# A hybrid attention and expert-retrieval layer on one core: sparse tiles normalised where each ends, the last four expert groups taken tile by tile

## The chip, the cores and the metric

The kernel runs on one core of one Trainium2 chip. The metric is the device time of one execution in microseconds (us), as the median of several runs. The engines are called as in the profile: PE is TensorE, whose weight loads stand apart as PEld, DVE is VectorE, ACT is ScalarE, POOL is GpSimd, and SP issues most of the DMAs.

## The reference

One layer over 1024 tokens of width 1024, all in f32. The first part (projection, gated linear attention, windowed attention, output projection and a layer norm) is not touched by the change. The second part is an expert mixer. Each token has 8 heads that each choose 16 of 16384 experts, so 128 chosen experts in all, and then a residual and a last layer norm follow:

```python
u = peer_u[eidx]
v = peer_v[eidx]
act = jax.nn.gelu(jnp.einsum('pd,phkd->phk', xt, u))
peer = jnp.einsum('phk,phkd->pd', gate * act, v)
x = _layernorm(alpha * x + g2 * peer, ln2_g[i], ln2_b[i])
```

## The kernel before, in words

The 1024 tokens are 8 tiles of 128. The kernel does the expert mixer in two ways at once.

**Dense tiles.** Tiles 0 to 4 (640 tokens) multiply with all 16384 experts, in 128 groups of 128. For each group `jj`, `products` loads the group's u-vectors, splits them into a high and a low part (ACT copy L901, DVE subtraction L902) and makes 2 x 24 matmuls of 320 columns (L115 to L117). `gated` applies Gelu (L1075), multiplies with the gates (L1077) and splits the result into the weights `W`. Every JG = 2 groups `outputs` loads the v-vectors through `values` (split by ACT L110 and DVE L111) and makes, for each of 5 tiles and 2 halves of the width, 6 matmuls of 512 columns into the PSUM tile `pyd`, which DVE adds to `yacc` in SBUF (L1105). The weights of two such pairs fit in SBUF at a time. The dense tokens themselves, `hhD`, stay in SBUF until the last product.

**Sparse tiles.** Tiles 5 to 7 take the 128 chosen experts of each token one by one, 128 steps a tile and 384 in all. A step gathers one row of 8 KB for each token (POOL's indirect DMA, L978, 1 MB), DVE multiplies and sums with the token (L995), ACT takes Gelu (L999) and scales the value half (L1011), and POOL adds it to `ys` (L1012). The gathers land in two rings of UB = 3 slots, six in all. A slot is allocated by `slot`, and `room` says whether one is free in program order. At step 96 of a tile `token` takes two slots to prepare the next tile.

**The order of work.** The program is written as one loop over `jj` (L1126 to L1138). After each half of `products` and each tile of `outputs`, `advance` takes as many sparse steps as are due: the 364 steps left are spread over SHARE = 0.98 of the dense work, measured in units in which a product half counts 0.25 and a pair of output groups counts 1. Each engine runs its own queue in order. A scheduler in the framework orders the instructions of the queues by its own simulation, so program order is not always queue order.

**The ends.** A finished sparse tile is stored to DRAM (`y_d`, L1020). After the products of the last group, `prepare` (L929) loads the three rows g2, l2g and l2b into the place of `hhD[0]`, the five residuals into the place of `hhD[1]`, and loads the stored sparse tiles again. `finish` (L948) then does an end: a product with g2 (L949), the residual and its sum (L951), the norm in `normalise` (L1168 to L1181) and the store (L953). In `normalise`, ACT squares and sums (L1171), POOL takes the power (L1173), and then either two DVE operations follow (L1175 and L1176, where FAST is 1) or one ACT operation, a POOL row (L1180) and another row by DVE or POOL (L1179 to L1181). Before the change FAST is 1 for tiles 3, 4 and 7, and SPLIT puts the g2 product and the last row of tiles 5 and 6 on POOL. The last pair of output groups, 126 and 127, runs tile by tile, each tile's end being written behind its second half.

Of the kernel before, what the change touches and what calls it, by code (L numbers as in the profile page):

```python
# [37 lines left out]
def kernel(ctx: ExitStack, tc: tile.TileContext, A, out):  # L38
# [888 lines left out]
    last, waiting = {}, []  # L927

    def prepare():  # L929

        rows = hd.tile([128, 3, D], F32, name="rows", tag="hhD0")
        base = hd.tile([128, 5, D], F32, name="base", tag="hhD1")
        for j in range(ND):
            if j < 3:
                name, src = (("g2", mod_d[3:4]), ("l2g", A["ln2_g"]), ("l2b", A["ln2_b"]))[j]
                last[name] = rows[:, j]
                spread(rows[:, j], src)
            last[j] = base[:, j]
            nc.sync.dma_start(base[:, j], xh_d[j])
        while waiting:  # L940
            j = waiting.pop(0)
            t, r = slot("late")
            r[0] = False
            nc.sync.dma_start(t[:, 0], y_d[j])
            nc.sync.dma_start(t[:, 1], xh_d[j])
            finish(j, t[:, 0], t[:, 1])

    def finish(j, y, x1):  # L948
        (V, G)[SPLIT[j]].tensor_tensor(y, y, last["g2"], OP.mult)  # L949
        mv = sx.tile([128, 2], F32, name="endmv", bufs=4)  # L950
        V.scalar_tensor_tensor(y, x1, ALPHA, y, OP.mult, OP.add, accum_out=mv[:, 0:1])  # L951
        normalise(nc, mhalf, y, x1, mv, last["l2g"], last["l2b"], FAST[j], (V, G)[SPLIT[j]])
        nc.sync.dma_start(out[128 * j:128 * j + 128, :], y)  # L953

    def sparse_steps():
# [25 lines left out]
        for n, (j, k) in enumerate(seq):  # L981
# [4 lines left out]
            while ahead[0] < len(seq) and ahead[0] - n + len(batch) < UB * len(rings) - (size - 1) and room():  # L986
                fetch()
# [9 lines left out]
            if len(batch) >= size or k == 127:  # L997
# [15 lines left out]
                batch.clear()  # L1013
            if k == 127:
                if last:
                    t, _ = slot("late")
                    nc.sync.dma_start(t[:, 0], xh_d[j])
                    finish(j, ys[j], t[:, 0])
                else:
                    nc.sync.dma_start(y_d[j], ys[j])  # L1020
                    waiting.append(j)
# [61 lines left out]
    def values(jj, n):  # L1083
        raw = ep.tile([128, 512], F32, tag="raw", name="vraw", bufs=7)
        nc.sync.dma_start(raw, A["uv"][128 * jj:128 * jj + 128, D + 512 * n:D + 512 * n + 512])
        hi = ep.tile([128, 512], F32R, name="vhi", bufs=4)
        lo = ep.tile([128, 512], F32R, name="vlo", bufs=4)
# [3 lines left out]
    def outputs(jjs, between):  # L1091
        final = jjs[-1] == NJ - 1
        todo = [(t, n) for t in range(ND) for n in range(2)] if final else [(t, n) for n in range(2) for t in range(ND)]
        for t, n in todo:
# [11 lines left out]
                if final and n:  # L1106
                    finish(t, yacc[:, t], last[t])
# [174 lines left out]
```

## Time and profile before

| what | us |
|---|---|
| median of 3 runs | 3180.56 |
| the three runs | 3179.79 to 3192.82 |
| the profiled execution's own time | 3178.78 |
| its span | 3177.0 |
| last matmul of `products` starts | 3108.87 |
| last matmul of all starts | 3130.82 |

The profiled execution is one run of the program. Its span is measured from its first to its last instruction, and 1.8 us of its time lie around it. Timelines and windows give times from the start of the span. A matmul's duration in the timeline overlaps with that of the next one, so the distance between two starts is what a matmul takes from the PE. "Idle before" names what the engine had waited for.

### The profile page before, as it was taken

The page shows a single profiled execution, that of the slowest core. Times are in us where ns is not written, and L with a number is a line of the kernel's source. Part 1 is how long each engine was busy: PE and PEld are TensorE (multiplying, and loading weights), DVE is VectorE, ACT ScalarE, POOL GpSimd, SP SyncE. Part 2 cuts the span into 40 slices and gives each one's busy share as a digit, 9 for nine tenths or more (in the row PEclk, how much of TensorE's full clock was granted, in tenths as well). Part 3 has the DMA queues.
Part 4 walks back from the last instruction along what each step waited for, and adds up shares of the span by engine and source line. Part 5 has one row for each costly group of instructions (what it writes and reads, how often), then busy time and mean ns, then how long its engine had stood idle before and what let it go on. Part 6 is the DMA issues. An engine that isn't in the chain of part 4 may idle for free. (4 is left out here: it accounts for less than half of the span.)

```text
span 3177.0 us, 48921 instructions
## 1 busy us (share of the span) xinstructions
PE 2829.0 (89%) x16604; PEld 2452.3 (77%) x16604; DVE 2594.7 (82%) x5684; ACT 1574.4 (50%) x3437; POOL 1679.8 (53%) x1111
## 2 busy tenths in 40 slices
PE   6998878879778887788999999999999999999893
PEld 3687756757578886677989888888888888888782
DVE  4318844578799999489988998999988999999898
ACT  3324545342547877734545554454544554445452
POOL 0012301052543543137776766778767777778676
PEclk8999879889889998999999999999999999999996
DMA  9653565646466566668898988989888998988884
GB/s 329 222 186 117 208 223 199 216 168 219 149 217 210 224 257 260 246 201 306 323 328 321 319 308 298 341 315 341 315 314 313 337 337 300 321 306 331 304 290 169
DMA packets 352679, 848.82 MB, mean 267 GB/s; under 512 B 27627, under 2 KB 165611, under 8 KB 299692
## 3 DMA queue, kind: packets, MB, share of 16 engines
q1 hardware_dynamic: 285520, 384.20, 36.9%
q0 software_dynamic: 55296, 402.68, 33.3%
q10 hardware_dynamic: 11612, 58.81, 4.8%
q8 instruction: 131, 2.15, 0.3%
q14 instruction: 120, 0.98, 0.1%
HBM read 745.43 MB, written 100.16 MB: 266 GB/s over the span
## 5 line engine op out<-in xcount | busy, mean ns | idle before, releaser
L1012 POOL TENSOR_TENSOR ys<-ys,uv 128x1024 f32<-128x1024 f32 x362 | 900.9, 2489 | 414.5 <-ACT uv L1011 386.9
L117 PE MATMUL pact<-hhD,ulo 128*128 128x320 f32 x2048 | 633.4, 316 | 48.7 <-DVE ulo L902 31.9
L115 PE MATMUL pact<-hhD,uhi 128*128 128x320 f32 x2048 | 641.5, 314 | 9.6 <-DVE W L111 7.4
L116 PE MATMUL pact<-hhD,uhi 128*128 128x320 f32 x2048 | 638.5, 313 | 0.0
L115 PE MATMUL pyd<-vhi,W 128*128 128x512 f32 x1280 | 515.2, 402 | 46.0 <-DVE yacc L1105 38.8
L978 POOL DMA_INDIRECT uv<-in_uv_dram,ex x384 | 415.5, 1082 | 223.0 <-issue 57.1
L116 PE MATMUL pyd<-vlo,W 128*128 128x512 f32 x1280 | 504.1, 394 | 0.2 <-DVE vlo L111 0.2
L117 PE MATMUL pyd<-vhi,W 128*128 128x512 f32 x1280 | 503.6, 397 | 0.0
L1011 ACT ACTIVATE uv<-uv,w 128x1024 f32<-128x1024 f32 x362 | 396.7, 1144 | 185.8 <-DVE w L1000 131.6
L995 DVE SCALAR_TENSOR_TENSOR uv<-uv,h2p 128x1024 f32<-128x1024 f32 x384 | 463.1, 1209 | 15.7 <-DMA uv<-in_uv_dram,ex 14.2
L1105 DVE TENSOR_TENSOR yacc<-yacc,pyd 128x512 f32<-128x512 f32 x630 | 417.3, 676 | 35.6 <-PE pyd L117 34.8
L117 PEld LDWEIGHTS pact<-hhD,ulo 128*128 128x128 f32 x2048 | 389.8, 192 | 68.8 <-DVE ulo L902 41.4
L115 PEld LDWEIGHTS pact<-hhD,uhi 128*128 128x128 f32 x2048 | 392.9, 192 | 24.4 <-DVE W L111 7.8
L116 PEld LDWEIGHTS pact<-hhD,uhi 128*128 128x128 f32 x2048 | 392.0, 191 | 10.7
L115 PEld LDWEIGHTS pyd<-vhi,W 128*128 128x128 f32 x1280 | 242.3, 189 | 94.5 <-DVE yacc L1105 47.4
L111 DVE TENSOR_TENSOR vlo<-vraw,vhi 128x512 fp32r<-128x512 f32 x256 | 284.0, 1131 | 12.2 <-ACT vhi L110 11.9
L902 DVE TENSOR_TENSOR ulo<-uraw,uhi 128x512 fp32r<-128x512 f32 x228 | 266.5, 1174 | 31.8 <-ACT uhi L901 30.4
L117 PEld LDWEIGHTS pyd<-vhi,W 128*128 128x128 f32 x1280 | 242.4, 190 | 58.4
L116 PEld LDWEIGHTS pyd<-vlo,W 128*128 128x128 f32 x1280 | 243.0, 190 | 39.6 <-DVE vlo L111 0.5
L832 PE MATMUL pgb<-ob,oa 128*128 128x128 f32 x1280 | 196.5, 299 | 51.5 <-ACT ob L828 33.8
L832 PEld LDWEIGHTS pgb<-ob,oa 128*128 128x128 f32 x1280 | 179.0, 202 | 65.7 <-ACT ob L828 50.9
L828 ACT ACTIVATE ob<-wb,gj 128x128 f32<-128x128 bf16 x640 | 210.5, 415 | 11.2 <-DVE wb L810 8.2
(357 smaller groups left out, 5099.9 us busy)
## 6 DMA issues: line engine op xcount, KB each, us to landing
uraw<-in_ut_dram SPq DMA_DIRECT2D x256, 256.0 KB, 5.3
vraw<-in_uv_dram SPq DMA_DIRECT2D x256, 256.0 KB, 8.4
g_d<-gstage ACTq DMA_DIRECT2D x20, 2048.0 KB, 6.4
gload<-g_d SPq DMA_DIRECT2D x32, 1280.0 KB, 13.7
wo<-wo_d SPq DMA_DIRECT2D x64, 512.0 KB, 6.1
wq<-wq_d SPq DMA_DIRECT2D x64, 512.0 KB, 6.6
wt<-in_w_ada_dram SPq DMA_DIRECT2D x48, 512.0 KB, 5.9
wq_d<-wqs SPq DMA_DIRECT2D x16, 512.0 KB, 6.0
```

The costliest lines, as they stand in the source:

```text
L111: eng.tensor_tensor(lo, src, hi.bitcast(F32), OP.subtract)
L115: PE.matmul(out_, l[0], r[0], start=(k == 0), stop=False)
L116: PE.matmul(out_, l[0], r[1], start=False, stop=False)
L117: PE.matmul(out_, l[1], r[0], start=False, stop=(k == n - 1))
L828: S.activation(o[1][:, c], w[:, :, c], AF.Copy, scale=gj[:, q + c:q + c + 1])
L832: PE.matmul(p[:, c::4], o[0][:, h + c], o[1][:, h + c], start=True, stop=True)
L902: lower.tensor_tensor(lo, raw, hi.bitcast(F32), OP.subtract)
L978: G.indirect_dma_start(out=uv[n][0].rearrange("p a d -> p (a d)"), out_offset=None, in_=A["uv"], in_offset=bass.IndirectOffsetOnAxis(ap=ch ...
L995: pin(V.scalar_tensor_tensor(t[:, 0], t[:, 0], 1.0, h2[j], OP.mult, OP.mult, accum_out=w[:, i:i + 1]))
L1011: S.activation(v, v, AF.Copy, scale=wb)
L1012: G.tensor_tensor(ys[j], ys[j], v, OP.add)
L1105: V.tensor_tensor(ya, ya, p, OP.add)
```

## The change

Three things are changed. A sparse tile no longer goes to DRAM. At its step 126 two slots of the rings are taken for the residual and the three rows of the norm, which are loaded then, and at step 127 its end runs at once, with the rows on POOL; the slots of tiles 5 and 6 are given back afterwards, those of tile 7 keep the rows for the dense ends. From step 120 of each sparse tile on, two gathers fewer are fetched ahead. The last four groups of outputs (124 to 127) are no longer two pairs but one pass, tile by tile, after all products and all sparse steps; the split values of groups 126 and 127 lie where `hhD[0]` was and the residuals where `hhD[1]` was. All five dense ends take the form with two DVE operations. SHARE goes from 0.98 to 0.96.

```diff
--- before.py
+++ after.py
@@ -924,33 +924,26 @@
     def spread(row, src):
         nc.scalar.dma_start(row, src.to_broadcast([128, D]))
 
-    last, waiting = {}, []
-
-    def prepare():
-
-        rows = hd.tile([128, 3, D], F32, name="rows", tag="hhD0")
-        base = hd.tile([128, 5, D], F32, name="base", tag="hhD1")
+    last, base, late = {}, {}, {}
+
+    def residuals():
+
+        rows = hd.tile([128, ND, D], F32, name="base", tag="hhD1")
         for j in range(ND):
-            if j < 3:
-                name, src = (("g2", mod_d[3:4]), ("l2g", A["ln2_g"]), ("l2b", A["ln2_b"]))[j]
-                last[name] = rows[:, j]
-                spread(rows[:, j], src)
-            last[j] = base[:, j]
-            nc.sync.dma_start(base[:, j], xh_d[j])
-        while waiting:
-            j = waiting.pop(0)
-            t, r = slot("late")
-            r[0] = False
-            nc.sync.dma_start(t[:, 0], y_d[j])
-            nc.sync.dma_start(t[:, 1], xh_d[j])
-            finish(j, t[:, 0], t[:, 1])
-
-    def finish(j, y, x1):
-        (V, G)[SPLIT[j]].tensor_tensor(y, y, last["g2"], OP.mult)
+            base[j] = rows[:, j]
+            nc.sync.dma_start(base[j], xh_d[j])
+        parts = hd.tile([128, 2 * JG, 2, 512], F32R, name="late", tag="hhD0")
+        for i in range(JG):
+            for n in range(2):
+                late[NJ - JG + i, n] = (parts[:, JG * n + i, 0], parts[:, JG * n + i, 1])
+
+    def finish(j, y, x1, fast, rows):
+        o = x1 if j >= ND else y
+        V.tensor_tensor(y, y, rows["g2"], OP.mult)
         mv = sx.tile([128, 2], F32, name="endmv", bufs=4)
-        V.scalar_tensor_tensor(y, x1, ALPHA, y, OP.mult, OP.add, accum_out=mv[:, 0:1])
-        normalise(nc, mhalf, y, x1, mv, last["l2g"], last["l2b"], FAST[j], (V, G)[SPLIT[j]])
-        nc.sync.dma_start(out[128 * j:128 * j + 128, :], y)
+        V.scalar_tensor_tensor(o, x1, ALPHA, y, OP.mult, OP.add, accum_out=mv[:, 0:1])
+        normalise(nc, mhalf, o, y if j >= ND else x1, mv, rows["l2g"], rows["l2b"], fast, G)
+        nc.sync.dma_start(out[128 * j:128 * j + 128, :], o)
 
     def sparse_steps():
 
@@ -983,7 +976,7 @@
             size = 1 if early else BATCH
             if n == 0 or k == 96 and j < NT - 1:
                 token(j + (k > 0))
-            while ahead[0] < len(seq) and ahead[0] - n + len(batch) < UB * len(rings) - (size - 1) and room():
+            while ahead[0] < len(seq) and ahead[0] - n + len(batch) < UB * len(rings) - (size - 1) - 2 * (k >= 120) and room():
                 fetch()
             if k == 0:
                 row, h2[j] = h2[j], ph.tile([128, D], F32, name="h2p", bufs=1)
@@ -1011,14 +1004,18 @@
                         S.activation(v, v, AF.Copy, scale=wb)
                         G.tensor_tensor(ys[j], ys[j], v, OP.add)
                 batch.clear()
+            if k == 126:
+                ends = [slot("late") for _ in range(2)]
+                (a, _), (b, _) = ends
+                x1 = a[:, 0]
+                last.update(g2=a[:, 1], l2g=b[:, 0], l2b=b[:, 1])
+                nc.sync.dma_start(x1, xh_d[j])
+                for name, src in (("g2", mod_d[3:4]), ("l2g", A["ln2_g"]), ("l2b", A["ln2_b"])):
+                    spread(last[name], src)
             if k == 127:
-                if last:
-                    t, _ = slot("late")
-                    nc.sync.dma_start(t[:, 0], xh_d[j])
-                    finish(j, ys[j], t[:, 0])
-                else:
-                    nc.sync.dma_start(y_d[j], ys[j])
-                    waiting.append(j)
+                finish(j, ys[j], x1, False, last)
+                for _, r in ends:
+                    r[0] = j == NT - 1
             yield
 
     with ExitStack() as gx:
@@ -1083,8 +1080,11 @@
     def values(jj, n):
         raw = ep.tile([128, 512], F32, tag="raw", name="vraw", bufs=7)
         nc.sync.dma_start(raw, A["uv"][128 * jj:128 * jj + 128, D + 512 * n:D + 512 * n + 512])
-        hi = ep.tile([128, 512], F32R, name="vhi", bufs=4)
-        lo = ep.tile([128, 512], F32R, name="vlo", bufs=4)
+        if (jj, n) in late:
+            hi, lo = late[jj, n]
+        else:
+            hi = ep.tile([128, 512], F32R, name="vhi", bufs=4)
+            lo = ep.tile([128, 512], F32R, name="vlo", bufs=4)
         split(hi, lo, raw)
         vals[jj, n] = hi, lo
 
@@ -1104,7 +1104,7 @@
                 else:
                     V.tensor_tensor(ya, ya, p, OP.add)
                 if final and n:
-                    finish(t, yacc[:, t], last[t])
+                    finish(t, yacc[:, t], base[t], True, last)
                 between()
 
     yacc = ep.tile([128, ND, D], F32, name="yacc")
@@ -1132,12 +1132,12 @@
                 acts[jj, h] = p
                 gated(jj, h)
                 advance(0.25)
-        if jj == NJ - 1:
-            prepare()
-        if jj % JG == 0 and jj:
+        if jj % JG == 0 and 0 < jj < NJ - JG:
             outputs(list(range(jj - JG, jj)), lambda: advance(JG / (4 * ND)))
     for _ in steps:
         pass
+    residuals()
+    outputs(list(range(NJ - 2 * JG, NJ)), lambda: None)
 
 
 PIECES = ((0, 1, 0, 8), (1, 1, 0, 4), (2, 2, 0, 2), (4, 4, 0, 1),
@@ -1155,14 +1155,12 @@
 UB = 3
 BATCH = 2
 FIRST = 20
-FAST = (0, 0, 0, 1, 1, 0, 0, 1)
-SPLIT = (0, 0, 0, 0, 0, 1, 1, 0)
 FILL = 3
 JG = 2
 GT = 32
 GG = 4
 GJ = 4
-SHARE = 0.98
+SHARE = 0.96
 
 
 def normalise(nc, mhalf, x, spare, mv, g, b, fast, end):
```

## Rows read from the trace of the kernel before

**Rows 1.** The page: the span, and busy time, share and instructions of each engine.

```profile
span 3177.0 us, 48921 instructions
...
PE 2829.0 (89%) x16604; PEld 2452.3 (77%) x16604; DVE 2594.7 (82%) x5684; ACT 1574.4 (50%) x3437; POOL 1679.8 (53%) x1111
```

**Rows 2.** Windows: width, busy PE PEld DVE ACT POOL (count), PEclk, DMA share, GB/s.

```profile
1900.00:3000.00 1100.00, 1059.46 (x5760) 944.25 (x5759) 1006.03 (x1575) 546.22 (x944) 818.65 (x461) 0.99 0.89 318
...
3109.00:3131.30 22.30, 17.22 (x62) 12.49 (x60) 17.04 (x24) 4.48 (x7) 13.06 (x5) 0.85 0.81 307
3131.30:3177.00 45.70, 0.00 (x0) 0.00 (x0) 38.95 (x47) 14.25 (x19) 28.51 (x15) 0.53 0.23 92
```

**Rows 3.** Waits, 1900 to 3000 us: total, times, longest.

```profile
PE pyd L115 <- DVE yacc L1105: 20.9, 13, 5.5
PE pact L117 <- DVE ulo L902: 19.3, 19, 2.0
```

**Rows 4.** Timeline of PE, 3108 to 3131 us: start, duration, instruction, idle before.

```profile
3108.72 0.31 PE L116 MATMUL pact<-hhD,uhi 128*128 128x320 f32 x1
3108.87 0.31 PE L117 MATMUL pact<-hhD,ulo 128*128 128x320 f32 x1
...
3109.26 0.40 PE L116 MATMUL pyd<-vlo,W 128*128 128x512 f32 x1
3109.49 0.40 PE L117 MATMUL pyd<-vhi,W 128*128 128x512 f32 x1
...
3121.57 0.79 PE L115 MATMUL pyd<-vhi,W 128*128 128x512 f32 x1 [3.60 <-DVE yacc L1105]
...
3130.82 0.39 PE L117 MATMUL pyd<-vhi,W 128*128 128x512 f32 x1
```

**Rows 5.** Timeline of DVE, 3134 to 3177 us.

```profile
3134.07 0.14 DVE L1178 TENSOR_TENSOR endmv<-endmv 128x1 f32<-128x1 f32 x1
3134.14 1.21 DVE L949 TENSOR_TENSOR yacc<-yacc,rows 128x1024 f32<-128x1024 f32 x1
...
3140.69 3.35 DVE L951 SCALAR_TENSOR_TENSOR yacc<-base,yacc 128x1024 f32<-128x1024 f32 x1
...
3156.93 1.22 DVE L951 SCALAR_TENSOR_TENSOR yacc<-base,yacc 128x1024 f32<-128x1024 f32 x1
...
3171.55 1.27 DVE L1176 SCALAR_TENSOR_TENSOR yacc<-yacc,endmv,rows 128x1024 f32<-128x1024 f32 x1
```

**Rows 6.** Timeline of POOL, 3112 to 3150 us.

```profile
3112.51 4.88 POOL L1012 TENSOR_TENSOR ys<-ys,uv 128x1024 f32<-128x1024 f32 x2 [1.99 <-ACT uv L1011]
...
3132.49 0.57 POOL L1173 TENSOR_TENSOR endmv<-endmv,mhalf 128x1 f32<-128x1 f32 x1 [6.03 <-DVE endmv L1172]
...
3142.92 6.59 POOL L1181 TENSOR_TENSOR late<-late,rows 128x1024 f32<-128x1024 f32 x2
```

**Rows 7.** Timeline of ACT in the last end.

```profile
3161.61 1.13 ACT L1171 ACTIVATE base<-yacc,endmv 128x1024 f32<-128x1024 f32 x1
```

**Rows 8.** Groups by line, 1900 to 3000 us: busy us, mean ns, idle before.

```profile
L1012 POOL TENSOR_TENSOR ys<-ys,uv 128x1024 f32<-128x1024 f32 x229 | 571.5, 2496 | 218.6 <-ACT uv L1011 197.1 <-ACT ys L1007 10.9 <-issue 1.1
...
L111 DVE TENSOR_TENSOR vlo<-vraw,vhi 128x512 fp32r<-128x512 f32 x156 | 176.8, 1154 | 8.6 <-ACT vhi L110 8.5
L902 DVE TENSOR_TENSOR ulo<-uraw,uhi 128x512 fp32r<-128x512 f32 x143 | 170.1, 1195 | 7.8 <-ACT uhi L901 6.8
```

**Rows 9.** The tile vraw over the run: duration ns min/median/max, first and last start.

```profile
L111 DVE TENSOR_TENSOR vlo<-vraw,vhi x256: 672/684/3234, 1338.2 to 3111.1; 128x512 fp32r<-128x512 f32 x128
```

**Rows 10.** The store of a finished sparse tile: duration, first and last start.

```profile
L1020 SPq DMA_DIRECT2D y_d<-ys x3: 319/326/327, 1901.6 to 3119.7; - x3
```

**Rows 11.** Timeline of POOL around the preparation of the last sparse tile.

```profile
2363.05 0.94 POOL L978 DMA_INDIRECT uv<-in_uv_dram,ex  x1 [10.72 <-DVE h2s L970]
```

**Rows 12.** Windows of the same stretch, columns as in rows 2.

```profile
2340.00:2362.00 22.00, 22.00 (x118) 19.42 (x117) 16.62 (x29) 8.74 (x16) 6.35 (x4) 1.00 0.74 290
```

**Rows 13.** The tile uv: its gathers from issue to landing, us.

```profile
DMA to landing us min/median/max: 5.3/8.2/12.5
```

## The prediction

> **What bounds the kernel now.** I read the page first, then windows by stage, then the waits of PE in the long stage, then the last 70 us engine by engine. The page shows PE busy for 89% of 3177.0 us and DVE for 82% [rows 1]. That is an average over two situations. In the long dense stage PE is busy for 1059 of 1100 us and DVE for 1006 [rows 2]: PE sets the pace, and the 40.5 us in which it is idle are almost all waits for DVE (20.9 and 19.3 us, [rows 3]). In the last 45.7 us PE has nothing left to do and DVE and POOL do eight norms [rows 2]. So two things count: the stretch from the last product's matmul to the end, 3109.0 to 3177.0, that is 68.0 us, and what the change adds to DVE in the long stage.
>
> In those 68.0 us the reader is to see three things. The last pair of outputs needs 60 matmuls; two starts lie 0.23 us apart [rows 4], so that is 13.8 us of PE, but it took 22.3 us at a granted clock of 0.85 [rows 2], among others because PE sat 3.60 us behind an add of DVE [rows 4]. DVE's residual step took 3.35 us while POOL worked on rows, and 1.22 us without them [rows 5, 6]. And no end was completed in the order of the tiles: DVE still did residual sums at 3140.69 and 3156.93, long after the last matmul at 3130.82 [rows 4, 5].
>
> **The change part by part.** I sum against the profiled span, with T = 3109.0 as the end of the last product.
>
> 1. *Four groups in one pass.* The 60 matmuls of groups 124 and 125, 13.8 us, move behind the last product: it ends 13.8 us earlier, and 120 x 0.23 = 27.6 us follow it instead of 13.8. PE's sum doesn't change. The adds of these groups are 10 instead of 20.
>
> 2. *Start of the pass.* Groups 124 and 125 cover 6 x 0.23 = 1.4 us. The values of 126 and 127 can be split only when `hhD[0]` is free, so ACT's copies and two DVE subtractions of 0.68 us [rows 9] start after the last product. I take a gap of 1.5 us. Below it is 0 (the first values in time); above it 8.5 us, what the last pair lost before (22.3 - 13.8 = 8.5, [rows 2]), which covers a value load or a residual load standing wrongly in SP's queue: the five residual loads wait there for `hhD[1]`, and whatever SP issues behind them waits too.
>
> 3. *Dense ends.* For one tile DVE now does two adds (0.68 each, as the same shape of [rows 9]), the g2 product 1.21, the residual 1.22, two small steps of 0.14, and two operations of 1.27 [rows 5]. That is 6.61 us; starts lie 0.07 us closer than durations say (3134.07 and 3134.14, [rows 5]), which takes off 8 x 0.07, and 6.05 us are left. PE needs 24 x 0.23 = 5.52 us a tile. So each end but the last hides behind the next tile's matmuls, and DVE is 4 x 0.53 = 2.1 us behind at the last one. The chain after the last matmul: 0.68 + 1.21 + 1.22 + 0.14, ACT's square 1.13 [rows 7], 0.14 + 1.27 + 1.27, less five overlaps of 0.07, is 6.7 us, and 0.5 us for handing over to ACT and back, an estimate. POOL's power, 0.57 us [rows 6], lies beside the first of the two last operations. The store came 4.2 us after DVE's last operation (3172.82 to 3177.0, [rows 1, 5]). Together 7.2 + 4.2 = 11.4 us.
>
> 4. *Sparse ends in the long stage.* Each adds to DVE 1.21 + 1.22 + 3 x 0.14 = 2.85 us, in all 8.6 us. Each adds two POOL rows like L1181's (3.3 us with DVE working, [rows 6]). What a POOL row costs DVE is seen in the long stage: subtractions take 1154 and 1195 ns instead of 684 [rows 8, 9], so 156 x 0.470 + 143 x 0.511 = 146 us over 229 POOL adds, 0.64 us each; six rows make 3.8 us. [...] Of 8.6 + 3.8 = 12.4 us I let half reach PE, 6.2, because neither engine is the bound alone (DVE idle 94 of 1100 us, PE 40, [rows 2]); the ends are 0 and 12.4. DMA's bytes stay the same (three stores and three reloads of sparse tiles go, six more row loads come). ACT's extra squares and issues lie in its idle half [rows 2].
>
> 5. *Two slots held.* The trace shows two slots taken once, when a tile is prepared: POOL stood 10.72 us [rows 11], PE stayed busy for all 22 us, and DVE for 16.6 of 22 [rows 12], 3.5 us less than its share in the long stage. Half of that, three times, is 5.2 us; the ends are 0 (PE lost nothing then) and 10.5. With two gathers fewer ahead, three steps of 4.76 us (1901.6 to 3119.7 over 256 steps, [rows 10]) stand against landings of 8.2, at most 12.5 us [rows 13], which still fits.
>
> 6. *SHARE 0.96.* Some seven steps leave the last stretch of the loop and are spread ahead of it. DVE's load rises there and falls behind by the same, each step about 2 us with its POOL add: net 0, ends 0 and +15 if what falls late is not regained.
>
> 7. *Tile 7's end.* Before, step 384 is due 8 pieces of output and one product before T (8 x 1.38 + 48 x 0.15 = 18 us), yet its POOL add ended at 3117.4 [rows 6], 26 us late. Now half a product, ten pieces and three products follow it, 38.4 us, so its add ends some 12 us before the last product, and its end may reach into the pass: 2 us, ends 0 and 7.
>
> Sum: 3109.0 - 13.8 + 6.2 + 5.2 = 3106.6 for the last product, + 1.5 + 27.6 + 2.1 + 11.4 + 2 = **3151.2** against 3177.0, so 25.8 us less. The median of the runs shown is 1.8 us above the profiled execution's own time (3180.56 against 3178.78); I take 25.8 us from the median: **3155 us**.
>
> **The rivals.**
>
> *A. DVE is the pace of the long stage.* For it: every wait of PE there is for DVE. Then the whole 12.4 + 10.5 + 15 = 37.9 us arrive instead of 11.4, and the time is 3181: no change. Against it: PE is busier than DVE. [...] Chance 0.17.
>
> *B. The ends still don't follow the tiles.* The last pair was tile by tile in the program before, too, and DVE's queue was ordered otherwise. If DVE does the finishing of five tiles after the last add, it needs 5 x 4.75 + 6 = 30 us behind PE in place of 13.5, and the time is 3171. Against it: what disordered it, late rows and reloads and POOL rows, is gone. Chance 0.14.
>
> *C. The sparse stream sets the pace.* If steps follow each other as fast as the ring allows, the stream's end stays at 3117.4 plus a pause p for each of tiles 5 and 6; the last product ends 12.4 us later and the span 44.6 us after that, at 3174.4 + 2p. With the 10.7 us of the pause that was seen [rows 11] this is 3195.8, a time of 3199: slower. It decides from p = 9.3 us on. For it: the end holds two slots longer than the preparation does, and DVE works in order, so a late gather stops the adds. Against it: PE ran through that pause. Chance 0.10.
>
> **How the numbers follow.** About 0.5% (16 us) is what a measurement of this kernel can tell from no change, so faster means under 3164.7 and slower over 3196.5. The forecast has 0.52, better than all its upper ends 0.07 (with steps 2, 4, 5 and 7 at their lower ends, 14.9 us less, 3140). Faster: 0.59 and 0.08 from the better parts of A and B, 0.67. Slower: C and a tail of A, 0.11. The rest, 0.22, is the same. The range is 3140 to 3190: its low end is the sum with the lower bounds, its high end takes in A, B and the milder half of C.
>
> **What would show it.** Right: the last product near 3107, matmuls at 0.23 us without a gap to about 3136, DVE's residual steps at 1.2 us in the order of the tiles, and 11 to 14 us between the last matmul and the end. Step 4 or 5 is wrong if PE's waits for DVE grow by more than 20 us, or PE stands still around the ends of tiles 5 and 6. Step 2 is wrong if PE's first wait in the pass is over 4 us or its clock falls. The forecast as a whole fails if the last product ends after 3120 or more than 25 us lie behind the last matmul.

## The result and the profile after

The changed kernel takes 3215.64 us (median of 6 runs, 3202.17 to 3223.82) against 3180.23 us for the kernel before (6 runs): a ratio of 1.0111, 95% interval 1.0086 to 1.0136. It is slower by 35 us where 25.8 us less were forecast, and it lies above the range. The profiled execution's own time is 3219.36 us, its span 3217.6.

The page of the changed kernel, against [rows 1]:

```profile
span 3217.6 us, 48884 instructions
...
PE 2849.5 (89%) x16604; PEld 2460.6 (76%) x16604; DVE 2637.9 (82%) x5675; ACT 1567.8 (49%) x3435; POOL 1673.7 (52%) x1108
```

The windows, with the columns of [rows 2]. The second is the time from the last product to the last matmul, the third what lies behind it:

```profile
1900.00:3000.00 1100.00, 1033.00 (x5538) 916.69 (x5537) 1006.49 (x1515) 523.32 (x908) 779.19 (x440) 0.98 0.85 304
3143.00:3176.20 33.20, 27.27 (x106) 20.51 (x104) 23.20 (x37) 12.98 (x20) 20.09 (x11) 0.90 0.68 269
3176.20:3217.60 41.40, 0.00 (x0) 0.00 (x0) 33.85 (x41) 8.14 (x13) 17.70 (x10) 0.54 0.19 76
```

The first row holds most of the answer. In the same 1100 us PE did 5538 matmuls instead of 5760 and was busy for 1033.0 us instead of 1059.5, while DVE was busy for exactly as long as before (1006.5 against 1006.0), with 60 instructions fewer. So a DVE instruction took longer on average. The waits of PE in that stretch, against [rows 3], and the groups, against [rows 8], say which:

```profile
PE pyd L115 <- DVE yacc L1105: 34.4, 26, 5.0
PE pact L117 <- DVE ulo L902: 30.4, 25, 2.7
```

```profile
L1005 POOL TENSOR_TENSOR ys<-ys,uv 128x1024 f32<-128x1024 f32 x216 | 538.9, 2495 | 251.1 <-ACT uv L1004 241.2 <-issue 1.2
...
L111 DVE TENSOR_TENSOR vlo<-vraw,vhi 128x512 fp32r<-128x512 f32 x150 | 189.9, 1289 | 12.2 <-ACT vhi L110 12.0
L902 DVE TENSOR_TENSOR ulo<-uraw,uhi 128x512 fp32r<-128x512 f32 x138 | 176.4, 1285 | 11.5 <-ACT uhi L901 8.5 <-PE pact L117 2.3
```

The same two waits grew by 24.6 us, and the subtractions from 1154 and 1195 to 1289 and 1285 ns. Above the 684 ns of an undisturbed one that is 150 x 0.605 + 138 x 0.601 = 174 us in the 1100, against 146 before, although POOL did 216 adds there instead of 229: 0.80 us for each add instead of 0.64. I call this sum the **excess** below; it is the number by which the experiments are compared.

By place: the last product began at 3142.7 instead of 3108.9 (forecast 3106.6), and 74.9 us lay behind it instead of 68.1 (forecast 44.6). What happened behind it shows in DVE's timeline, against [rows 5]:

```profile
3171.28 1.21 DVE L988 SCALAR_TENSOR_TENSOR uv<-uv,h2p 128x1024 f32<-128x1024 f32 x1
...
3174.06 8.94 DVE L942 TENSOR_TENSOR yacc<-yacc,late 128x1024 f32<-128x1024 f32 x4
...
3185.79 1.21 DVE L944 SCALAR_TENSOR_TENSOR late<-late,ys 128x1024 f32<-128x1024 f32 x1
...
3186.93 1.22 DVE L944 SCALAR_TENSOR_TENSOR yacc<-base,yacc 128x1024 f32<-128x1024 f32 x1
...
3204.46 1.22 DVE L944 SCALAR_TENSOR_TENSOR yacc<-base,yacc 128x1024 f32<-128x1024 f32 x1
```

The last step of the sparse stream (L988) came at 3171.3, 64 us later than before and inside the pass. Tile 7's residual (the row with `late<-late,ys`) followed at 3185.8, and the first dense residual stands directly behind it, though four dense tiles were summed by 3174. POOL's timeline shows the stream's last add and the two pauses of its gathers (L971) at the ends of tiles 5 and 6:

```profile
1904.96 1.82 POOL L971 DMA_INDIRECT uv<-in_uv_dram,ex  x1 [0.30 <-issue]
1911.04 0.57 POOL L1171 TENSOR_TENSOR endmv<-endmv,mhalf 128x1 f32<-128x1 f32 x1 [4.26 <-DVE endmv L1170]
1914.88 1.00 POOL L971 DMA_INDIRECT uv<-in_uv_dram,ex  x1 [3.27 <-ACT ys L1000]
...
2564.35 1.42 POOL L971 DMA_INDIRECT uv<-in_uv_dram,ex  x1 [0.30 <-issue]
...
2582.74 1.01 POOL L971 DMA_INDIRECT uv<-in_uv_dram,ex  x1 [3.34 <-ACT ys L1000]
...
3174.26 6.52 POOL L1005 TENSOR_TENSOR ys<-ys,uv 128x1024 f32<-128x1024 f32 x2 [7.25 <-ACT uv L1004]
```

From gather to gather 9.9 and 18.4 us went by, where the kernel before had 6.2 and 11.8 at the same places. Gaps of such a length stand elsewhere, too: the longest before is 20.1 us, from 1934.6. The last add ended at 3180.8, 38 us after the last product; the forecast had it 12 us before.

### The profile page after: what moved, and what is told of

Read it like the earlier page. It is cut to its first block, busy times and chain, and to the rows that moved or that the text cites. A ratio compares the mean times of both kernels' runs of the same rounds, so it can differ in the third digit from the quotient of the medians.

```text
span 3217.6 us, 48884 instructions
## 1 busy us (share of the span) xinstructions
PE 2849.5 (89%) x16604; PEld 2460.6 (76%) x16604; DVE 2637.9 (82%) x5675; ACT 1567.8 (49%) x3435; POOL 1673.7 (52%) x1108
## 4 chain that ended last, share of the span: by engine, by line
DVE 33%; PE 29%; issue 10%; ACT 8%; DMA 6%; POOL 1%; SPq 1%; DVEq 0%; ACTq 0%; POOLq 0%
DVE uv L988 5%; DVE vlo L111 5%; DVE ulo L902 4%; DVE yacc L1105 4%; PE pyd L115 4%; PE pact L117 3%; PE pact L116 3%; PE pyd L116 3%; PE pyd L117 3%; PE pact L115 3%; ACT uv L1004 2%; DMA gload<-g_d 2%; DVE oa L824 2%; DVE W L111 1%; PE po_att L576 1%
## 5 line engine op out<-in xcount | busy, mean ns | idle before, releaser
L1005 POOL TENSOR_TENSOR ys<-ys,uv 128x1024 f32<-128x1024 f32 x362 | 904.6, 2499 | 438.6 <-ACT uv L1004 421.4
L115 PE MATMUL pyd<-vhi,W 128*128 128x512 f32 x1260 | 510.3, 405 | 54.5 <-DVE yacc L1105 47.5
L971 POOL DMA_INDIRECT uv<-in_uv_dram,ex x384 | 416.5, 1085 | 230.4 <-issue 57.5
L117 PE MATMUL pyd<-vhi,W 128*128 128x512 f32 x1260 | 497.3, 398 | 1.7 <-DVE W L111 1.7
L116 PE MATMUL pyd<-vlo,W 128*128 128x512 f32 x1260 | 497.2, 395 | 0.0
L988 DVE SCALAR_TENSOR_TENSOR uv<-uv,h2p 128x1024 f32<-128x1024 f32 x384 | 462.3, 1208 | 12.2 <-DMA uv<-in_uv_dram,ex 11.3
L1105 DVE TENSOR_TENSOR yacc<-yacc,pyd 128x512 f32<-128x512 f32 x620 | 410.5, 676 | 30.4 <-PE pyd L117 29.8
L116 PEld LDWEIGHTS pact<-hhD,uhi 128*128 128x128 f32 x2048 | 394.5, 193 | 10.9
L111 DVE TENSOR_TENSOR vlo<-vraw,vhi 128x512 fp32r<-128x512 f32 x252 | 318.8, 1289 | 22.2 <-ACT vhi L110 22.1
L902 DVE TENSOR_TENSOR ulo<-uraw,uhi 128x512 fp32r<-128x512 f32 x228 | 274.2, 1208 | 38.0 <-ACT uhi L901 34.5
L110 ACT ACTIVATE W<-pact 128x320 fp32r<-128x320 f32 x222 | 95.3, 432 | 327.7 <-DVE pact L1074 324.5
```

What stands on the lines that cost most here:

```text
L110: S.activation(hi, src, AF.Copy)
L111: eng.tensor_tensor(lo, src, hi.bitcast(F32), OP.subtract)
L115: PE.matmul(out_, l[0], r[0], start=(k == 0), stop=False)
L116: PE.matmul(out_, l[0], r[1], start=False, stop=False)
L117: PE.matmul(out_, l[1], r[0], start=False, stop=(k == n - 1))
L902: lower.tensor_tensor(lo, raw, hi.bitcast(F32), OP.subtract)
```

## The experiments

Three theories stood after this reading; the expectations below call them by these numbers. Theory 1: the slots held by a sparse end, and the order of the queues behind it, make DVE's subtractions stand behind POOL's adds. Theory 2: SHARE = 0.96 does it alone, by a stream of steps that is 2% denser. Theory 3: the sparse stream has a pace of its own, whatever SHARE says. Letters stand for narrower questions: A and B ask what holds the dense ends (rows that come late, or their place behind tile 7's in DVE's queue), R whether the ring's slots set the stream's pace, L whether POOL's adds are what is lost, S whether the end of the stream and then DVE's ends set the finish.

For each profiled run I give the ratio to the kernel before on the same chip, the excess and PE's busy time in 1900 to 3000 us (before: 146 us and 1059.5 us), and where it matters the length of the long stage, from add 20 to add 590 into `yacc` (before 1598.4 us, after 1654.0). Adds and steps are counted from 0, and the ten copies that open `yacc` count as adds.

**SHARE alone, each way.** The changed kernel with the old value:

```diff
-SHARE = 0.96
+SHARE = 0.98
```

> The changed kernel with SHARE 0.98 again, nothing else. Theory 1 (the slots held by a sparse end, and the order of the queues behind it, make DVE's subtractions stand behind POOL's adds in tile 6's stretch): the long stage stays some 40 to 50 us late and the time near 3215. Theory 2 (a stream of steps 2% denser overloads DVE): most of the loss goes, 3165 to 3185. Theory 3 (the sparse stream has a pace of its own, about 4.75 us a step, whatever SHARE says): the last step stays within 15 us of 3171 and the time within 10 us of 3215.

And the kernel before with the new one:

```diff
-SHARE = 0.98
+SHARE = 0.96
```

> The kernel before with SHARE 0.96, nothing else. Theory 1: no change, 3175 to 3190. Theory 2: 3200 or more. Theory 3: the last step stays within 10 us of 3107, dense work is merely displaced, and the time is within 10 us of 3180.

The changed kernel with 0.98 took 3188.07 us, ratio 1.0031 (1.0014 to 1.0047): stage 1609.4 us, excess 165, PE 1053.3. The kernel before with 0.96 took 3197.17 us, ratio 1.0060 (1.0038 to 1.0081): stage 1632.6 us, excess 160, PE 1048.8. The windows of the two, 0.98 first:

```profile
1900.00:3000.00 1100.00, 1053.32 (x5714) 940.43 (x5713) 1015.92 (x1566) 543.34 (x940) 806.37 (x452) 0.99 0.88 316
```

```profile
1900.00:3000.00 1100.00, 1048.80 (x5652) 933.54 (x5652) 1006.76 (x1543) 538.53 (x926) 800.18 (x449) 0.99 0.87 311
```

3188 lies just above what Theory 2 expected and far from the 3215 of the others; 3197 lies between what Theories 1 and 2 expected. So none of the three holds as it was put: SHARE costs by itself, and the rest of the change isn't free. The groups and waits of the kernel before with 0.96, in the same stretch:

```profile
L902 DVE TENSOR_TENSOR ulo<-uraw,uhi 128x512 fp32r<-128x512 f32 x139 | 182.3, 1322 | 14.1 <-ACT uhi L901 11.4 <-PE pact L117 2.2
L111 DVE TENSOR_TENSOR vlo<-vraw,vhi 128x512 fp32r<-128x512 f32 x154 | 173.2, 1147 | 10.0 <-ACT vhi L110 9.9
```

```profile
PE pact L117 <- DVE ulo L902: 30.5, 25, 3.5
PE pyd L115 <- DVE yacc L1105: 19.7, 16, 2.5
```

One constant moved `ulo` from 1195 to 1322 ns, and PE's wait for it from 19.3 to 30.5 us, with no instruction more. In the long stage 0.96 costs 34 us alone and 45 us with the sparse ends (1654.0 - 1609.4); the sparse ends cost 11 us at 0.98 and 21 at 0.96. Of this less is left at the end of the kernel: by the ratios 0.96 costs 19 us alone (1.0060) and 25 us with the sparse ends (1.0111 against 1.0031).

**Is it how dense the steps stand, or one unlucky order?** The same constant at the values beside it, in the kernel before:

```diff
-SHARE = 0.98
+SHARE = 0.97
```

(and 0.99, 0.95)

> The kernel before with SHARE 0.97. If the loss at 0.96 (3197) comes from steps packed denser, this lies about halfway, 3186 to 3191. If SHARE only draws another order of the queues and the order decides how often DVE's subtractions stand behind POOL's adds: any value from 3165 to 3200, not on that line, and DVE's lost time per POOL add in the three tiles' stretches goes with the time.

> The kernel before with SHARE 0.99. Density: 3170 to 3178, faster than before. Order alone: any value from 3165 to 3200.

> The kernel before with SHARE 0.95. If a smaller SHARE costs more the smaller it is: 3203 or more, DVE's lost time between add 20 and add 590 above the 314 us of share96. If 0.96 is one unlucky order among several: below 3192, with lost time below 305 us. In both cases the steps stand at the same adds as before (591 to 593 adds before step 360).

0.97 gave 1.0018 (1.0005 to 1.0031), excess 148, PE 1059.4; 0.99 gave 0.9981 (0.9964 to 0.9997), 142, 1061.9; 0.95 gave 1.0005 (0.9990 to 1.0020), 145, 1056.6. So 0.96 is worse than the values on both sides of it. A density would grow from 0.99 to 0.95, and this doesn't; 0.97 and 0.99 alone would not decide it (3175.18 lies in both ranges expected for 0.99), but 0.95 came 24 us below what a density asks. And the steps don't get denser: 592 adds were done before step 360 at 0.95, 0.97, 0.98 and 0.99, and 591 at 0.96.

What a value of SHARE changes is the order in which instructions stand in the queues. The traces show it: DVE's instructions from add 20 to add 590 follow each other in another order at each of the five values. Where two kernels have the same order there, they have nearly the same stage. The order, by tile and operation, is the same in the kernel before and in the two kernels with its long stage below (dense ends alone; pass without held slots): 1598.4, 1592.9 and 1593.8 us. It is the same in the four kernels with all sparse ends and 0.98: 1609.1 to 1611.5 us. And it is the same in the two kernels with 0.96 and no sparse end in the stage: 1632.6 and 1632.0 us. The orders of 0.95, 0.97 and 0.99 took 1608.7, 1614.5 and 1610.8 us, so 0.98 was the best of the five here.

**The ends of tiles 5 and 6 left out**, from the changed kernel at 0.96:

```diff
-            while ahead[0] < len(seq) and ahead[0] - n + len(batch) < UB * len(rings) - (size - 1) - 2 * (k >= 120) and room():
+            while ahead[0] < len(seq) and ahead[0] - n + len(batch) < UB * len(rings) - (size - 1) - 2 * (k >= 120 and j == NT - 1) and room():
...
-            if k == 126:
+            if k == 126 and j == NT - 1:
...
-            if k == 127:
+            if k == 127 and j == NT - 1:
```

> The changed kernel without the ends of tiles 5 and 6, which are left out together with their slots and with the shorter fetching ahead; tile 7 and the dense tiles keep theirs. Tiles 5 and 6 are not written. Theory 1: the slow stretch of tile 6 goes, the last product comes near 3095 to 3105 instead of 3142.7, and the time is 3160 to 3175. Theories 2 and 3: the last product stays later than 3125 and the time above 3195.

3172.26 us, ratio 0.9981 (0.9961 to 1.0000). The stage was 1627.3 us, 26.7 less than in the changed kernel, but still 29 above the kernel before: excess 164, PE 1050.0. The last step came at 3118.6 instead of 3171.3, tile 7's residual at 3132.6, the first dense one at 3133.8. The time lies in the range of Theory 1, the last product, at 3117.1, doesn't: it was expected at 3095 to 3105. Without the two ends, 589 adds were done before step 360, with them 599: the two ends, with the slots that they hold, push the stream back by ten adds against the dense work.

**The pass put back to two pairs**, with SHARE 0.98, sparse ends and fast dense ends kept:

```diff
-        parts = hd.tile([128, 2 * JG, 2, 512], F32R, name="late", tag="hhD0")
...
-        if jj % JG == 0 and 0 < jj < NJ - JG:
+        if jj == NJ - 1:
+            residuals()
+        if jj == NJ:
+            for _ in steps:
+                pass
+        if jj % JG == 0 and jj:
             outputs(list(range(jj - JG, jj)), lambda: advance(JG / (4 * ND)))
...
-    residuals()
-    outputs(list(range(NJ - 2 * JG, NJ)), lambda: None)
```

> The changed kernel with the last four groups as two pairs again and SHARE 0.98: sparse ends where each ends and dense ends without POOL rows remain. Theory 1: still some 40 us late before the last product, the time 3190 to 3220. If the four-group pass itself is the loss: 3150 to 3175, since the rows of the dense ends are there and the ends are short.

3196.18 us, ratio 1.0061 (1.0035 to 1.0086); stage 1609.1 us, excess 166. The last product came 10.9 us later than with the pass at the same SHARE (3126.0 against 3115.1), but the end only 2.0 us later in the profile (3188.9 against 3186.9), because tile 7's residual moved by 2.0 (3157.1 against 3155.1). The pass's gain before the last product is there. In the profiled executions it doesn't reach the end; by the medians (3196.18 against 3188.07, with intervals of the ratios that overlap) it may, so this stays open.

**What orders the dense ends.** With SHARE 0.98, first the dense ends get rows of their own, so that they no longer share tile 7's (the five residuals then share two places):

```diff
-    last, base, late = {}, {}, {}
+    last, base, late, own = {}, {}, {}, {}
...
+        for i, (name, src) in enumerate((("g2", mod_d[3:4]), ("l2g", A["ln2_g"]), ("l2b", A["ln2_b"]))):
+            own[name] = rows[:, i]
+            nc.sync.dma_start(own[name], src.to_broadcast([128, D]))
...
-                    finish(t, yacc[:, t], base[t], True, last)
+                    finish(t, yacc[:, t], base[t], True, own)
```

> As share98 (3188), but the dense ends take their three rows from the place of hhD, loaded after the last product, with the residuals of tiles 2 to 4 loaded behind those of 0 to 2; tile 7 keeps its own rows. Theory A (the dense ends wait for rows that come only at tile 7's step 126): the end comes 15 to 20 us earlier, 3165 to 3175. Theory B (the dense residual sums stand in DVE's queue behind that of tile 7, whatever the rows do): only the five g2 products move ahead, 3 to 8 us, and dense residuals still begin right behind tile 7's; 3179 to 3187.

Then tile 7's end is also written behind the dense ends:

```diff
-                finish(j, ys[j], x1, False, last)
...
+                    tail.append((j, ys[j], x1))
...
+    for j, y, x1 in tail:
+        finish(j, y, x1, False, last)
```

> As ownrows, with tile 7's end written behind the dense ends in the program. Theory B: the dense ends run beside the last steps, and what is left behind tile 7's last POOL add is its own end, some 20 us instead of 33: 3165 to 3176. Theory A: no difference to ownrows beyond 4 us.

Own rows gave 1.0040 (1.0027 to 1.0054): tile 7's residual at 3155.6, the first dense one at 3156.8, as before. The rows were not what held them. The second edit gave 1.0034 (1.0023 to 1.0046), and the order of DVE's residuals turned round:

```profile
3133.66 2.68 DVE L948 SCALAR_TENSOR_TENSOR yacc<-base,yacc 128x1024 f32<-128x1024 f32 x1
...
3167.61 1.21 DVE L948 SCALAR_TENSOR_TENSOR yacc<-base,yacc 128x1024 f32<-128x1024 f32 x1
...
3171.15 1.21 DVE L948 SCALAR_TENSOR_TENSOR late<-late,ys 128x1024 f32<-128x1024 f32 x1
```

The first dense residual came 23 us earlier, but the end stayed at 3188.2. Now the last step stood behind dense work (3154.4 instead of 3142 at the same SHARE) and tile 7's residual was the last. So Theory B names the order rightly, but both times lie above what it expected: the order alone gained nothing, because the stream still ended late.

**What sets the stream's pace.** The kernel before with one gather fewer ahead:

```diff
-            while ahead[0] < len(seq) and ahead[0] - n + len(batch) < UB * len(rings) - (size - 1) and room():
+            while ahead[0] < len(seq) and ahead[0] - n + len(batch) < UB * len(rings) - (size - 1) - (not early) and room():
```

> The kernel before with one gather fewer fetched ahead in the long stage, four in place of five. Theory R (the six slots set the stream's own pace, so that neither SHARE nor anything else brings steps forward): a step takes 5.5 us or more in place of 4.76, the last step comes far later than 3107, and the time rises by 50 us or more. If the slots are not the limit: steps stay at 4.7 to 4.9 us and the time within 15 us of 3180.

3324.18 us, ratio 1.0462 (1.0425 to 1.0499). DVE's waits for gathers in 1900 to 3000 us and the row of the steps' line:

```profile
DVE uv L995 <- DMA uv<-in_uv_dram,ex: 24.8, 21, 3.0
```

```profile
L995 DVE SCALAR_TENSOR_TENSOR uv<-uv,h2p x384: 1200/1210/1223, 1081.7 to 3267.8; 128x1024 f32<-128x1024 f32 x192
```

Before, that wait was 5.5 us and the last step started at 3107.3. From step 40 to step 360 a step took 5.28 us instead of 4.78. One slot costs the stream 0.50 us a step, somewhat less than expected, and 160 us at its end. The waits for gathers grew by only 19 us in the 1100; the rest is order: 614 adds were done before step 360 instead of 592. So the ring's slots limit the stream's pace, and a smaller SHARE, which writes the steps earlier into the program, didn't bring them forward. No run had a slot more.

**POOL's adds taken out**, from the kernel before (L1012) and from the changed one (L1005), nothing else:

```diff
                         S.activation(v, v, AF.Copy, scale=wb)
-                        G.tensor_tensor(ys[j], ys[j], v, OP.add)
```

> The kernel before without POOL's adds of the sparse values (L1012 left out, so the sparse tiles' outputs lack nearly all of their experts). Theory L (DVE sets the pace of the long stage, and what it loses behind POOL's adds goes into the time one to one): subtractions fall to 0.69 us, the loss of 277 us between add 20 and add 590 to under 40, and the stage shortens until PE is the bound, by 50 to 90 us; the time is 3090 to 3130. If POOL is hidden: within 15 us of 3180.

> The changed kernel without the same adds. Theory L: the extra 56 us of the long stage go too, so that it lies within 15 us of before_noadd, or below it. If the sparse ends, the slots or SHARE cost the time in another way than by POOL's adds: 25 us or more above before_noadd.

3100.74 us and 3074.35 us, ratios 0.9759 (0.9724 to 0.9793) and 0.9676 (0.9641 to 0.9710). The windows of 1900 to 2900 us, the kernel before without adds first:

```profile
1900.00:2900.00 1000.00, 997.41 (x5491) 898.56 (x5490) 794.59 (x1501) 530.54 (x900) 209.66 (x220) 1.00 0.92 335
```

and the changed kernel without adds, with its two groups:

```profile
1900.00:2900.00 1000.00, 995.53 (x5488) 897.34 (x5487) 798.45 (x1507) 526.00 (x900) 212.22 (x221) 1.00 0.92 335
```

```profile
L111 DVE TENSOR_TENSOR vlo<-vraw,vhi 128x512 fp32r<-128x512 f32 x148 | 99.0, 684 | 9.0 <-ACT vhi L110 8.8
L902 DVE TENSOR_TENSOR ulo<-uraw,uhi 128x512 fp32r<-128x512 f32 x136 | 92.9, 686 | 20.8 <-ACT uhi L901 17.9 <-issue 1.8
```

All subtractions take their 684 ns, PE is busy for over 99% of the time in both kernels, and here, with SHARE 0.96, sparse ends and held slots in it, the changed kernel is the faster one, by 26.4 us. So it loses its time only beside POOL's adds. The edit does one thing more: without the add a slot comes free once ACT has scaled it, and a step took 4.62 us instead of 4.78 (from step 40 to step 360 of the kernel before). It is therefore not shown that the longer subtractions are the whole of the loss.

**The pass without held slots.** From the kernel before: the pass of four groups and dense ends in two DVE operations with rows of their own; tiles 5 and 6 through DRAM as before, and all three sparse ends, in two DVE operations as well, written behind the dense ones; SHARE 0.98.

```diff
-        if jj == NJ - 1:
-            prepare()
-        if jj % JG == 0 and jj:
+        if jj % JG == 0 and 0 < jj < NJ - JG:
             outputs(list(range(jj - JG, jj)), lambda: advance(JG / (4 * ND)))
...
+    residuals()
+    for j in range(ND, NT - 1):
+        t, r = slot("late")
+        nc.sync.dma_start(t[:, 0], y_d[j])
+        nc.sync.dma_start(t[:, 1], xh_d[j])
+        tail.append((j, t[:, 0], t[:, 1]))
+    outputs(list(range(NJ - 2 * JG, NJ)), lambda: None)
+    for j, y, x1 in tail[1:] + tail[:1]:
+        finish(j, y, x1, True, own)
```

> The pass of four groups and the dense ends of the change (own rows in the place of hhD), but sparse tiles 5 and 6 go through DRAM as before and all three sparse tiles are ended behind the dense ends, with two DVE operations each; no slots are held in the long stage; SHARE 0.98. Theory S (the end of the stream and then DVE's ends set the finish, and ends in the long stage only push the stream back): the last product near 3097, the last step within 10 us of 3107, the end near 3155, a time of 3152 to 3168. If the pass itself is of no use: 3172 or more.

3161.77 us, ratio 0.9944 (0.9928 to 0.9960): faster than both kernels. Its window, its last adds on POOL, and its first and last dense and its last sparse residual:

```profile
1900.00:3000.00 1100.00, 1063.67 (x5797) 948.51 (x5796) 1012.73 (x1587) 552.12 (x955) 820.03 (x460) 0.99 0.89 320
```

```profile
3106.36 11.61 POOL L1009 TENSOR_TENSOR ys<-ys,uv 128x1024 f32<-128x1024 f32 x4 [4.93 <-ACT uv L1008]
```

```profile
3116.23 2.82 DVE L948 SCALAR_TENSOR_TENSOR yacc<-base,yacc 128x1024 f32<-128x1024 f32 x1
...
3139.78 1.23 DVE L948 SCALAR_TENSOR_TENSOR yacc<-base,yacc 128x1024 f32<-128x1024 f32 x1 [0.95 <-DMA base<-xh_d]
...
3150.76 1.22 DVE L948 SCALAR_TENSOR_TENSOR late<-late,ys 128x1024 f32<-128x1024 f32 x1
```

The long stage is that of the kernel before (excess 149, stage 1593.8 us), the last product came at 3098.3, 10.5 us earlier than before, and the stream's last add ended 20 us behind it. Is the gain the edit's or the order's? The same kernel at 0.96 and at 1.0:

```diff
-SHARE = 0.98
+SHARE = 0.96
```

> pass_late (3162) with SHARE 0.96 in place of 0.98, no sparse end in the long stage. If SHARE 0.96 costs by itself: 3174 to 3190, and DVE's lost time rises from 282 to some 310 us. If it cost only together with the sparse ends: 3155 to 3168.

> pass_late with SHARE 1.0. If the loss grows as SHARE falls: 3150 to 3160, faster than pass_late. If the order alone decides: 3155 to 3180, on either side.

1.0039 (1.0025 to 1.0054) and 1.0043 (1.0027 to 1.0058): each some 30 us above 0.98 by the ratios, at 0.96 with an excess of 163 and a stage of 1632.0 us:

```profile
1900.00:3000.00 1100.00, 1046.56 (x5645) 931.34 (x5645) 1010.48 (x1546) 537.62 (x924) 795.97 (x447) 0.99 0.87 311
```

At 0.98 DVE's order in the long stage is that of the kernel before, so the gain there is the edit's: 0.9944 against 1. At 0.96, again with one and the same order, it is 1.0039 against 1.0060, with intervals that overlap. So the lead over the kernel before holds only at the better order. At 1.0 both expected ranges were missed. The excess was 142 and the stage 1624.6 us, so there the loss is of another kind: 600 adds were done before step 360, and DVE waited 31.9 us for loads of the gates (`gload`) instead of 10.3. I didn't follow it up.

**The fast dense ends alone**, in the kernel before:

```diff
-FAST = (0, 0, 0, 1, 1, 0, 0, 1)
+FAST = (1, 1, 1, 1, 1, 0, 0, 1)
```

> The kernel before with the dense ends of the change alone: all five with two DVE operations and no POOL row (FAST). The long stage is not touched. If POOL's rows delay DVE in the last 46 us: two or three residual sums at 1.2 in place of 3.35 us and 4 to 10 us off the end, 3170 to 3176. If the end is set by tile 7's late reload alone: 3177 to 3182.

3175.86 us, ratio 1.0002 (0.9985 to 1.0019). Three residuals still took 3.35 us, as [rows 5] has them; the first of them:

```profile
3138.74 3.35 DVE L951 SCALAR_TENSOR_TENSOR yacc<-base,yacc 128x1024 f32<-128x1024 f32 x1
```

POOL's rows of tiles 5 and 6 (two of 6.59 us together, from 3140.97) lie beside them. So the rows beside the long residuals are not those of the dense tiles, and taking these away changed nothing that the ratio shows, though 4 to 10 us were expected.

## Why the prediction was wrong

Both marks named for the forecast as a whole showed: the last product came at 3142.7, not before 3120, and 41.8 us, not 25 at most, lay behind the last matmul (3175.8 to 3217.6).

**The step that failed first is 6** (SHARE 0.96: net 0, ends 0 and +15). It had the steps spread more densely, their load given back later. They don't move (591 adds against 592 before step 360), since the ring's slots limit the stream's pace; what moves is the order of the queues. In the long stage that cost 34 us alone and 45 us in the changed kernel, and 19 and 25 us were left in the time, outside the bound that was set. The bound came from the load that SHARE moves, and a new order has no such bound. The description of the change counts three things; this constant is a fourth.

**Step 7 failed as well**: tile 7's last add was to end 12 us before the last product and ended 38 us after it. (The step's own terms give 39.0 us of work behind the last step, not 38.4, which matters little.) It reckoned by due places in the program; but from 0.95 to 0.99 a step of the kernel before took 4.8 to 4.9 us whatever was due, and the two ends put the stream further back (ten adds). This step and the order of the dense ends would have failed the forecast without step 6, too: with 0.98 put back, the profiled span still misses the 3151.2 us by 35.7 us, 8.5 of them at the last product and 27.1 behind it.

**Steps 4 and 5** gave 6.2 + 5.2 = 11.4 us; at SHARE 0.98 the stage grew by 11.0 (1598.4 to 1609.4). The nearness proves little: the orders of 0.95, 0.97 and 0.99, without any sparse end, grew it by 10 to 16. The path was right only in part: the excess grew by 18 to 20 us in all four kernels with sparse ends and 0.98 (165 to 166 against 146), far more than four POOL rows explain (2.6 us at the 0.64 us of step 4). At 0.96 the same ends cost 21 to 27 us. The mark set for these steps, PE's waits for DVE up by more than 20 us, showed with 24.6; of that the ends alone gave 5.8 (27.0 and 19.0 us at 0.98) and 0.96 alone 10.0, the rest came with both together.

**"Half of it reaches PE"** in step 4 failed as a rule. From before to after the excess grew by 27.3 us and PE's busy time fell by 26.5: it arrived one to one. With 0.96 against 0.98 it was 13.6 and 10.7 us in the kernel before, 13.7 and 17.1 in the pass without held slots. But in the four kernels with sparse ends and 0.98 PE lost 5 to 8 us of those 18 to 20, about a third, and the whole 146 us of the kernel before stand against 40.5 idle us of PE. So there is no fixed share. Rival A (DVE is the pace of the long stage, and the whole arrives) was given 0.17 because PE is the busier engine. Its mechanism came true for the change as a whole (its time, 3181, didn't), not for the ends alone. A busy share doesn't decide this: DVE's busy time was 1006 us in both kernels while the work done in it fell.

**Rival C** had the mechanism of the late stream and the sign, with a chance of 0.10. In its terms the last add stays at 3117.4 plus 2p. It ended at 3153.8 with 0.98 and at 3180.8 in the changed kernel, so 2p was 36 and 63 us, more than the 21.4 that it took, though the pauses without a gather grew by only 10 us together (9.9 and 18.4 against 6.2 and 11.8). Where it erred is the place: it had the last product wait for the stream, and the last product went ahead of it by 38 us, so that only a part of the stream's delay reached the end. With 0.98 the change came out at 1.0031; to 3199 it would not have come alone, and with the other order it came to 3215.6.

**Rival B** (0.14) was right on the order: the dense ends didn't follow the tiles. Wherever tile 7's end is written first, the first dense residual stands directly behind tile 7's (3139.5 and 3140.7 before; 3185.8 and 3186.9 after; 3155.1 and 3156.2 at 0.98; 3132.6 and 3133.8 without the ends of tiles 5 and 6), and the end comes 32 to 38 us behind tile 7's. What orders them was said to be gone (late rows, reloads, POOL rows); it was the place in the program, as writing tile 7's end last showed. With that undone nothing was gained, because the stream still ended late.

**Step 2** took a gap of 1.5 us; it was 4.31, within its bound of 8.5 but wrong by the mark set for it (over 4 us). PE's granted clock was 0.90 in the pass as a whole, 0.50 from 3148.0 to 3152.5 us and 1.00 from there on: right behind the wait two starts lay 0.43 us apart (3149.65 and 3150.08), later 0.23. PE waited for ACT's copies of the last values:

```profile
3148.02 1.83 PE L115 MATMUL pyd<-late,W 128*128 128x512 f32 x3 [4.31 <-ACT late L110]
```

**Step 1 and the prices of step 3** stand. With the pass the stretch from add 590 to the last product took 94.5 us, with two pairs 108.3, both at 0.98: the 13.8 us that step 1 said. The last product came 10.9 us earlier. Matmuls came at 0.23 us once past the wait, and dense residuals without a POOL row beside them took 1.21 or 1.22 us. The 0.5 us for handing over to ACT and back was taken from no row; at the last square but one DVE stood idle for 1.30 us around ACT's square, which the step puts at 1.13, so it was under 0.2:

```profile
3208.30 0.15 DVE L1170 TENSOR_SCALAR endmv<-endmv 128x1 f32<-128x1 f32 x1 [1.30 <-ACT base L1169]
```

**Step 3's overlap failed.** Each end but the last was to hide behind the next tile's matmuls; all five dense residuals came behind the last matmul (3175.8), the first at 3186.9, for the reason given under Rival B.

The whole, without POOL's adds, gave 26.4 us where 25.8 were forecast. That is luck, since it is split otherwise: in the profiled spans 16.8 us before the last product (3036.3 to 3019.5) and 8.1 behind it (62.3 to 54.2), not 2.4 and 23.4.

**The account of the 35 us**, in the profiled spans: +40.6 = +33.8 at the last product and +6.8 behind it. The first is 55.6 us of long stage, of which 11 came with the sparse ends and 45 with 0.96 on top of them, less 15.6 by which the stretch from there to the last product was shorter (107.2 to 91.6, the pass's gain) and less 6.2 by which the stage began earlier. The second is the tail's saving, eaten by a stream that ends 38 us after the last product.

**What stays open.** That another order of the queues goes with another length of the stage is shown. Why the subtractions lose more beside POOL's adds in the order of 0.96 is only argued: no run held the order fixed and moved an add. That dense residuals keep the program's place behind tile 7's is shown, what in the scheduling makes it so is not. Neither the loss at 1.0 nor what the pass is worth at the end of the changed kernel was followed up.

## What to carry to other kernels

Where a scheduler orders the queues, a tuned constant is a draw: here one of its values cost 0.6% between neighbours within 0.2%, and the value before the change was the best draw of five in the long stage. So try the values beside it before a gain or loss is put down to an edit, and keep such a constant out of a change of something else. Before work is moved to the end of a stream, find what limits that stream's pace (here the slots of its ring), and count what holds them. Where one engine's instructions are lengthened by another's, don't price what reaches the critical engine at a fixed share: here it went from a third to all of it with the order of the queues, however busy the two were on average. Put both ends into the range, and read the share from the critical engine's busy time in a run.

## What the runs showed that I had not expected

POOL's adds of the sparse stream cost this kernel 78 us of 3179 (ratio 0.9759 without them), though POOL is busy for half the time only. The DVE instructions that lose most time by them are the subtractions with both inputs in SBUF: 684 ns without the adds, 1118 to 1322 ns with them (means of the two groups over the runs). DVE's adds with an input in PSUM took 676 ns with them and 682 without, and the steps of line L988, which read the token's row from PSUM, 1208 and 1211 ns.

The trace of the kernel before has the same one by one, from 1900 to 3000 us. Of the 299 subtractions 117 took more than 0.8 us, 1.94 on average; each of these lay beside an add of POOL and ended 0.55 to 0.56 us after that add did. The other 182 took 0.68 us, though 21 of them lay beside an add for a part of their time. Of DVE's 388 adds from PSUM 192 lay beside an add of POOL, and none took more than 0.69 us.

The excess ran from 142 to 174 us in 1100 for nearly the same work, and it went with the order of the queues.
